# A gelu-times-half kernel: the first two tiles in pieces, later tiles in whole instructions, activations pinned in order

## Chip, cores, metric

One core of one Trainium2 chip. The metric is the device time of one execution in microseconds (us); lower is better. Every run below except two slow executions of one experiment is in the fast state, and only fast runs are compared. A ratio is the mean time of one kernel's fast runs over the mean of the kernel before's fast runs of the same rounds, on the same chip; it is not quite the ratio of the medians quoted beside it. The span of a profile, from its first to its last instruction, is some 2 us shorter than the time.

## The reference

```python
def setup_inputs():
    batch, seq, dim = (32, 512, 2048)
    return {'x': np.random.randn(batch, seq, dim).astype(np.float32)}

def reference(x):
    half_dim = x.shape[-1] // 2
    x1, x2 = x[..., :half_dim], x[..., half_dim:]
    gelu_x1 = 0.5 * x1 * (1 + erf(x1 / np.sqrt(2)))
    return (gelu_x1 * x2).astype(np.float32)
```

134.2 MB are read and 67.1 MB written, and there is one gelu and one product for each output element.

## The kernel before

The input is cut into 16 tiles. In a tile each of the 128 partitions holds R = 8 rows, so a load moves 8.39 MB (64 KB contiguous per partition) and a store 4.19 MB (32 KB per partition). There are two input and two output buffers. The gelu runs in place on the left half of the input tile (ACT), the product goes into the output tile (DVE). Loads are issued on the SP queue, stores on the ACT queue, except those of the last two tiles, which are on the SP queue behind the last load.

```python
R = 8
xpool = ctx.enter_context(tc.tile_pool(name="xpool", bufs=2))
opool = ctx.enter_context(tc.tile_pool(name="opool", bufs=2))

def load(i):
    x_tile = xpool.tile([P, R, dim], x.dtype, name="x_tile")
    nc.sync.dma_start(out=x_tile, in_=x_t[i])
    return x_tile

def store(queue, i, o_tile, rows):
    queue.dma_start(out=o_t[i][:, rows, :], in_=o_tile[:, rows, :])

ahead = [load(0), load(1)]
for i in range(n_tiles):
    x_tile = ahead.pop(0)
    o_tile = opool.tile([P, R, half], out.dtype, name="o_tile")
    last = i == n_tiles - 1
    for lo, hi in ((0, 1), (1, 2), (2, 4), (4, 8)) if last else ((0, 4), (4, 8)):
        rows = slice(lo, hi)
        nc.scalar.activation(
            out=x_tile[:, rows, :half], in_=x_tile[:, rows, :half], func=GELU
        )
        nc.vector.tensor_mul(
            out=o_tile[:, rows, :], in0=x_tile[:, rows, :half], in1=x_tile[:, rows, half:],
        )
        if last and hi % 4 == 0:
            store(nc.sync, i, o_tile, slice(hi - 4, hi))
    if not last:
        store(nc.sync if i == n_tiles - 2 else nc.scalar, i, o_tile, slice(0, R))
    if i + 2 < n_tiles:
        ahead.append(load(i + 2))
# ... launch code cut
```

The instructions pass a scheduler when the program is built. It may put an instruction of an engine ahead of another that was written earlier. The written order is therefore not always the order on the engine.

Of the kernel before, what the change touches and what calls it, by code (L numbers as in the profile page):

```python
# [1 line left out]

# [4 lines left out]

GELU = mybir.ActivationFunctionType.Gelu


@with_exitstack
def kernel(
    ctx: ExitStack,
    tc: tile.TileContext,
    x: bass.AP,
    out: bass.AP,
):






    nc = tc.nc
    P = nc.NUM_PARTITIONS

    x_flat = x.flatten_outer_dims()
    out_flat = out.flatten_outer_dims()
    n_rows, dim = x_flat.shape
    half = dim // 2  # L30

    R = 8
    x_t = x_flat.rearrange("(n p r) d -> n p r d", p=P, r=R)
    o_t = out_flat.rearrange("(n p r) d -> n p r d", p=P, r=R)
    n_tiles = x_t.shape[0]
# [9 lines that stand above are left out]
    def store(queue, i, o_tile, rows):  # L45
        queue.dma_start(out=o_t[i][:, rows, :], in_=o_tile[:, rows, :])

    ahead = [load(0), load(1)]
    for i in range(n_tiles):
        x_tile = ahead.pop(0)  # L50
        o_tile = opool.tile([P, R, half], out.dtype, name="o_tile")
        last = i == n_tiles - 1
        for lo, hi in ((0, 1), (1, 2), (2, 4), (4, 8)) if last else ((0, 4), (4, 8)):
            rows = slice(lo, hi)
            nc.scalar.activation(  # L55
                out=x_tile[:, rows, :half], in_=x_tile[:, rows, :half], func=GELU
            )
            nc.vector.tensor_mul(  # L58
                out=o_tile[:, rows, :],
                in0=x_tile[:, rows, :half],  # L60
                in1=x_tile[:, rows, half:],
            )
            if last and hi % 4 == 0:
                store(nc.sync, i, o_tile, slice(hi - 4, hi))
        if not last:
            store(nc.sync if i == n_tiles - 2 else nc.scalar, i, o_tile, slice(0, R))
        if i + 2 < n_tiles:
            ahead.append(load(i + 2))


# [1 line left out]
_INS = ['x']  # L72
_OUTS = [((32, 512, 1024), 'float32')]


# [23 lines left out]
```

## Time and profile before

| | before |
|---|---|
| time, median of the 3 runs given at the start | 471.6 us (471.53 to 471.65) |
| span of the profile | 470.1 us |
| DVE / ACT busy | 140.5 / 115.4 us |
| bytes over the span | 201.3 MB, 428 GB/s |
| in the middle (tiles 3 to 13) | 434 GB/s, 29.0 us a tile |

How to read it: busy shares tell little here, because ACT and DVE work in short bursts between landings (7.12 and 8.76 us in each 29.0 us of the middle). The question is whether the transfer engines ever stand still, and that is answered by the byte rate in windows cut where tiles land. The prediction below shows those lines.

### The profile page before, as it was taken

How to read it: one execution, taken by the hardware profiler on the slowest of the kernel's cores; microseconds unless marked ns; L12 is line 12 of the kernel's file. 1: busy time of each engine (PE TensorE's matmuls, PEld its weight loads, DVE VectorE, ACT ScalarE, POOL GpSimd, SP SyncE). 2: the span in 40 equal slices, each digit the busy share in tenths (PEclk: the TensorE clock that was granted, in tenths of full speed). 3: DMA queues.
4: the chain of work that ended last, by engine and by line, in shares of the span. 5: the costliest groups of instructions: out<-in, count | busy, mean ns of one | idle time of the engine just before them, and what ended most of it. 6: DMA issues, size and time to landing. Idle time of an engine off the chain costs nothing.

```text
span 470.1 us, 217 instructions
## 1 busy us (share of the span) xinstructions
DVE 140.5 (30%) x34; ACT 115.4 (25%) x35; POOL 0.2 (0%) x4
## 2 busy tenths in 40 slices
DVE  0070703307043070420705106061150601507042
ACT  1051406024060230603206032060410605105060
POOL 0000000000000000000000000000000000000000
DMA  8999999999999999999999999999999999999988
GB/s 357 446 446 357 443 449 446 402 443 449 402 446 441 435 457 404 432 418 485 407 424 421 488 407 413 432 488 407 402 443 482 413 402 443 472 424 402 480 380 346
DMA packets 4754, 201.35 MB, mean 428 GB/s; under 512 B 528, under 2 KB 528, under 8 KB 528
## 3 DMA queue, kind: packets, MB, share of 16 engines
q1 hardware_dynamic: 2736, 142.61, 70.5%
q10 hardware_dynamic: 2016, 58.72, 28.9%
q14 instruction: 2, 0.02, 0.0%
HBM read 134.22 MB, written 67.11 MB: 428 GB/s over the span
## 4 chain that ended last, share of the span: by engine, by line
DMA 77%; DVE 14%; ACT 7%; issue 0%; ACTq 0%; SPq 0%
DMA x_tile<-in_x_dram 77%; DVE o_tile L58 14%; ACT x_tile L55 7%; ACTq L94 0%; SPq L42 0%; ACTq L55 0%
## 5 line engine op out<-in xcount | busy, mean ns | idle before, releaser
L58 DVE TENSOR_TENSOR o_tile<-x_tile 128x4096 f32<-128x4096 f32 (+2 forms) x34 | 140.5, 4171 | 321.2 <-ACT x_tile L55 321.2
L55 ACT ACTIVATE x_tile<-x_tile 128x4096 f32<-128x4096 f32 (+2 forms) x34 | 114.2, 3407 | 341.0 <-DMA x_tile<-in_x_dram 341.0
L55 ACT ACT_TABLE_LOAD x1 | 1.3, 1283 | 0.7 <-PEq L83 0.7
L83 POOL MEMSET const-bfloat16-1.0<- 128x1 bf16 x1 | 0.1, 102 | 0.0
L83 POOL MEMSET const-uint8-127<- 128x1 uint8 x1 | 0.1, 102 | 0.0
L83 POOL MEMSET const-float32-0.0<- 128x1 f32 x1 | 0.1, 99 | 0.2 <-issue 0.2
L83 POOL MEMSET const-float32-1.0<- 128x1 f32 x1 | 0.1, 99 | 0.0
## 6 DMA issues: line engine op xcount, KB each, us to landing
out_dram<-o_tile ACTq DMA_DIRECT2D x14, 4096.0 KB, 41.6
out_dram<-o_tile SPq DMA_DIRECT2D x1, 4096.0 KB, 24.8
out_dram<-o_tile SPq DMA_DIRECT2D x2, 2048.0 KB, 8.0
x_tile<-in_x_dram SPq DMA_DIRECT2D x16, 45.4
```

The lines of the kernel that those rows point to most:

```text
L55: nc.scalar.activation(out=x_tile[:, rows, :half], in_=x_tile[:, rows, :half], func=GELU)
L58: nc.vector.tensor_mul(out=o_tile[:, rows, :], in0=x_tile[:, rows, :half], in1=x_tile[:, rows, half:],)
L83: nc = _bacc.Bacc("TRN2", target_bir_lowering=False, num_devices=1)
```

## The change

Its intent: compute and store sooner at the start by cutting the loads, the instructions and the stores of tiles 0 and 1 into pieces; then pay less fixed cost by covering a whole tile with one activation and one product; and keep each activation behind the store written ahead of it (`keep_in_program_order`, called the pin below).

```diff
-    ahead = [load(0), load(1)]
+    def load_pieces(i):
+        x_tile = xpool.tile([P, R, dim], x.dtype, name="x_tile")
+        for r in range(0, R, 4):
+            rows = slice(r, r + 4)
+            nc.sync.dma_start(out=x_tile[:, rows, :], in_=x_t[i][:, rows, :])
+        return x_tile
+
+    ahead = [load_pieces(0), load_pieces(1)]
     for i in range(n_tiles):
...
-        for lo, hi in ((0, 1), (1, 2), (2, 4), (4, 8)) if last else ((0, 4), (4, 8)):
+        pieces = last or i < 2
+        if last or i == 0:
+            steps = (0, 1), (1, 2), (2, 4), (4, 8)
+        else:
+            steps = ((0, 4), (4, 8)) if i == 1 else ((0, 8),)
+        for lo, hi in steps:
             rows = slice(lo, hi)
-            nc.scalar.activation(
-                out=x_tile[:, rows, :half], in_=x_tile[:, rows, :half], func=GELU
+            tc.keep_in_program_order(
+                nc.scalar.activation(
+                    out=x_tile[:, rows, :half], in_=x_tile[:, rows, :half], func=GELU
+                )
             )
...
-            if last and hi % 4 == 0:
-                store(nc.sync, i, o_tile, slice(hi - 4, hi))
-        if not last:
+            if pieces and hi % 4 == 0:
+                store(nc.sync if last else nc.scalar, i, o_tile, slice(hi - 4, hi))
+        if not pieces:
             store(nc.sync if i == n_tiles - 2 else nc.scalar, i, o_tile, slice(0, R))
```

## The prediction

> **What bounds the kernel now.** I read the page from the top: the busy shares of the engines, the slices, the queues, then the chain that ended last, and asked the windows for the byte rate stage by stage.
>
> From the page of the kernel before:
>
> ```profile
> DVE 140.5 (30%) x34; ACT 115.4 (25%) x35; POOL 0.2 (0%) x4
> ...
> DMA  8999999999999999999999999999999999999988
> ...
> HBM read 134.22 MB, written 67.11 MB: 428 GB/s over the span
> ...
> DMA 77%; DVE 14%; ACT 7%; issue 0%; ACTq 0%; SPq 0%
> ```
>
> No compute engine is busy a third of the time; the transfer engines are at 90% or more in all but the first and the last two slices. The chain gives DVE and ACT 21%, but that is a walk back through releases: it crosses them because a load is issued when a buffer comes free, not because the transfers stood still meanwhile. Whether they stood still is a question for the windows, cut where tiles land (columns: window, its length, DVE, ACT and POOL busy with counts, clock, DMA share, GB/s):
>
> ```profile
> 0.00:22.80 22.80, 0.00 (x0) 1.29 (x2) 0.20 (x4) 1.00 0.98 414
> 22.80:45.19 22.39, 8.76 (x2) 7.12 (x2) 0.00 (x0) 1.00 1.02 413
> ...
> 103.35:422.35 319.00, 96.37 (x22) 78.36 (x23) 0.00 (x0) 1.00 1.00 434
> 422.35:449.89 27.54, 8.76 (x2) 7.12 (x2) 0.00 (x0) 1.00 0.96 415
> 449.89:461.70 11.81, 9.08 (x4) 7.31 (x4) 0.00 (x0) 1.00 0.97 416
> 461.70:470.10 8.40, 0.00 (x0) 0.00 (x0) 0.00 (x0) 1.00 0.74 318
> ```
>
> The middle runs at 434 GB/s, tile after tile: 8.39 MB in and 4.19 MB out are 12.58 MB, over 434 that is 29.0 us, the spacing of the activations below. All 201.33 MB at 434 GB/s take 463.9 us of the 470.1 us span. So 6.2 us is everything that is not transfer at the middle's rate. The head: 414 x 22.8 + 413 x 22.39 = 18.7 MB by 45.19 us, which at 434 needs 43.1 us, so it costs 2.1 us. The other 4.1 us are at the end: some 2 us are the last wait for completion and the finish (the last store is issued at 461.7 and lands 7.6 us later, the shortest of the stores, at 469.3; the span ends 0.8 us after), and some 2 us are rates of 415 rather than 434 from 422 us on. These short windows count whole packets (64 KB on each of 16 engines is 1 MB), so the split is good to a microsecond or two.
>
> The buffers turn over like this (timeline: start, us, engine, line, op, count, idle before and releaser):
>
> ```profile
> 22.80 7.12 ACT L55 ACTIVATE x_tile<-x_tile 128x4096 f32<-128x4096 f32 x2 [20.79 <-DMA x_tile<-in_x_dram]
> 26.45 8.76 DVE L58 TENSOR_TENSOR o_tile<-x_tile 128x4096 f32<-128x4096 f32 x2 [26.45 <-ACT x_tile L55]
> 35.24 0.38 ACTq L46 DMA_DIRECT2D out_dram<-o_tile  x1
> 45.19 7.12 ACT L55 ACTIVATE x_tile<-x_tile 128x4096 f32<-128x4096 f32 x2 [15.27 <-DMA x_tile<-in_x_dram]
> ...
> 74.42 7.12 ACT L55 ACTIVATE x_tile<-x_tile 128x4096 f32<-128x4096 f32 x2 [22.10 <-DMA x_tile<-in_x_dram]
> ...
> 103.35 7.12 ACT L55 ACTIVATE x_tile<-x_tile 128x4096 f32<-128x4096 f32 x2 [21.81 <-DMA x_tile<-in_x_dram]
> ```
>
> Tile 0 lands at 22.8, its product is done 12.4 us later, and then load 2 and store 0 go out. Load 1 still has 10 us to run: the load queue is never empty. In the middle the next load has 29.0 - 12.4 = 16.6 us left when a buffer comes free. The idle time of ACT and DVE costs nothing.
>
> [...] load 2, against stores with half its packet size, took 29.2 us (45.19 to 74.42), or 287 GB/s, two thirds of 434; equal bytes would have given it about 217 while a store ran. [...]
>
> **The change part by part.**
>
> *Loads of tiles 0 and 1 in two pieces.* Two more issues at 0.33 us, ahead of any need; no byte more or less. The first piece is 4.19 MB, 9.7 us: from the head's 2.1 us it is through at 11.8. In the kernel before load 0 should be through at 2.1 + 19.3 = 21.4 and ACT starts at 22.8, so I add 1.4 us for completion: ACT starts at 13.2 instead of 22.8.
>
> *Steps of tile 0.* Activations of 1, 1 and 2 rows (1049, 1049 and 1895 ns, as the last tile has them) end near 17.1, the 2-row product of 2.29 us at 19.4. Store 0a goes out at 19.4; in the old kernel the first store went at 35.2. Rows 4 to 8 land at about 22.8 as before, then 3.6 + 4.4 us: store 0b and load 2 go at 30.9 instead of 35.2. That is 4.3 us earlier, into a queue that holds load 1 anyway.
>
> *The pinned activation.* The activation of rows 4 to 8 stays behind the issue of store 0a (19.4 to 19.8). Its data come at 22.8, so the pin costs nothing. For later tiles the store waits for a product that ends long before the next tile lands.
>
> *Sharing afterwards.* From 21 us stores take a third. Load 1a and store 0a (32 KB against 16 KB packets) run to about 36, load 1b and store 0b to about 50.4; tile 1 is finished at 51.8 + 8.1 = 59.9 (57.6 before). Store 1 now moves in 16 KB packets against load packets of 64 KB, four to one: load 2 is through near 74.6 and load 3 near 98.8, four us ahead of before (about 102). Store 1 ends there too, and from then on the ratio is two to one, 29.0 us a tile.
>
> *Whole-tile instructions.* [...] In sequence 15.7 us, where two overlapped pieces took 12.4: 3.3 us later for each store and each load, 13 tiles (2 to 14). [...] The next load has 29.0 - 15.7 = 13.3 us left at the issue, so none of the 3.3 us reaches the transfer engines. Even if a load had all of them to itself it would take 19.3 us, above 15.7. The output buffer is not a wait either: store i ends about when load i+2 lands, and product i+2 starts 7.0 us after that.
>
> *The end.* Last tile unchanged; store 14 sits on the load queue behind load 15, and stores 14 and 15 are 8.39 MB, 19.3 us of transfers after the last load, against 11.8 us of compute until the last issue. It was covered before (449.9 to 469.3 is 19.4) and is covered now.
>
> *Sum.* Bytes: 0. Head until the first byte: 0. The stretch of loads alone gets some 15 us shorter; the windows of 5 us from 5 to 35 average 430 GB/s against 434 mixed, so this is worth 15 x 4/434 = 0.14 us. [...] The end is shifted in phase: store 13 now ends with load 15, not 2 us ahead of it, and part of the 2 us of poorer rate there may come back or grow. I take a gain of 0.4 us as the middle: 471.6 - 0.4 = 471.2.
>
> **The rivals.** *A: the earlier start carries through.* If the head counted as latency, the 4.3 us by which load 2 goes earlier would come off (467.3), or the 9.6 us of ACT (462.0). For it: the chain has 21% compute. Against it: 418 to 434 GB/s in the windows while that compute runs, and the 463.9 us of bytes, which leave no room[...]. *B: the longer compute empties the load queue.* Then up to 3.3 us on 13 tiles, 43 us: 514. Against it: 13.3 us of queued load, and 19.3 against 15.7 in the worst case. *C: a wait for the output buffer.* Store 1's small packets end it late; product 3 would start at about 107 and store 1 ends near 99, a margin of 7 us; a miss would delay load 5's issue, still covered. About 471.5. *D: smaller descriptors lower the rate.* The stores' 32 KB packets run inside the 434, and only 25 MB are concerned; even 3% worse there is 1.7 us: 473. *E: the end loses its cover*, if phases shift so that an engine runs dry before the last store: 1 or 2 us, 473.
>
> **Range and chances.** The middle follows from a floor of 463.9 us, which the change cannot touch, with 6 to 7 us around it of which perhaps 2 can move. So 470.3 to 472.3 for 8 in 10: half a load packet's round at the low side, D and E in part at the high side. [...] Slower by over 2% (481) needs B in part: 2%. Within: 97%.
>
> **What would show it.** Right: first store near 19.4 us, activation of tile 0 near 13, load 2 at about 31, activations in the middle 29.0 us apart with 434 GB/s, whole-tile durations of 7.0 and 8.7 us, time to landing of loads down from 45.4 to about 42 and of stores near 42, load share unchanged; DMA row full from slice 2 to 38. Wrong: a spacing over 29.1 us, a window of the middle under 425 GB/s, DVE waiting on stores, or a last load that lands more than 3 us from 449 us. If the time falls below 469, my account of the head or of the end is wrong; if it rises above 474, rate or queue.

The sum came to a gain of 0.4 us, 471.6 - 0.4 = 471.2; the 0.4 was a guess at the middle.

The 15.7 us in sequence are 7.0 for the activation of a whole tile and 8.7 for its product. The trace of the kernel before gives the same as an estimate: activations of 2048 and 4096 elements take 1895 and 3608 ns, so 8192 take 3608 + 2 x 1713 = 7034; products take 2293 and 4422, so 4422 + 2 x 2129 = 8680. Two neighbouring activations of 4096 overlap a little (7.12 us for both). That sharing goes by packet size, four to one as well as two to one, is an estimate from load 2 of the kernel before (29.2 us, 287 of 434 GB/s). That the transfers can't go faster than the 434 GB/s of the middle (the "floor of 463.9 us") is an estimate too.

## The result

| | before | after |
|---|---|---|
| time, median (6 runs each) | 471.56 us (471.34 to 471.69) | 471.81 us (471.71 to 472.17) |
| ratio | | 1.0007, 95% interval 0.9994 to 1.002 |
| span of the profile | 470.1 us | 469.6 us |

The two kernels take the same time as far as these runs can tell.

From the page of the kernel after (busy time of the engines, the slices, the bytes, the chain):

```profile
DVE 140.0 (30%) x23; ACT 114.6 (24%) x24; POOL 0.2 (0%) x4
...
DMA  8999999999999999999999999999999999999998
...
HBM read 134.22 MB, written 67.11 MB: 429 GB/s over the span
...
DMA 70%; DVE 14%; ACT 12%; another core or an unknown queue 1%; ACTq 0%; issue 0%; SPq 0%
```

There are 22 fewer compute instructions, and the transfer row is as full as before. ACT's share of the chain rose from 7% to 12%, since the chain now runs through a whole-tile activation, and the time did not move.

The windows of the kernel after, cut where its tiles land (window, length, DVE, ACT and POOL busy with counts, clock, DMA share, GB/s):

```profile
0.00:22.73 22.73, 4.66 (x3) 5.08 (x4) 0.20 (x4) 1.00 0.95 392
22.73:52.20 29.47, 8.85 (x2) 7.23 (x2) 0.00 (x0) 1.00 1.03 445
...
129.62:420.04 290.42, 86.92 (x10) 70.29 (x10) 0.00 (x0) 1.00 1.00 433
420.04:449.37 29.33, 8.69 (x1) 7.03 (x2) 0.00 (x0) 1.00 0.95 411
449.37:461.20 11.83, 9.08 (x4) 7.31 (x4) 0.00 (x0) 1.00 1.01 436
461.20:469.60 8.40, 0.00 (x0) 0.00 (x0) 0.00 (x0) 1.00 0.75 322
```

Ten tiles take 290.42 us, 29.04 a tile at 433 GB/s; the kernel before takes 29.00 at 434. Compute work now lies in the first window, and the end has the same shape. The first window's 392 GB/s (414 before) is made good by the second: 22.0 MB are through by 52.20 us, which at 434 GB/s need 50.8 us. So the head costs 1.4 us against 2.1 before, a difference below what these windows resolve.

The timeline of the kernel after (start, us, engine, line, operation, count, idle before and releaser; ACTq and SPq are issues of transfers on the queue of ACT or SP):

```profile
12.89 3.80 ACT L69 ACTIVATE x_tile<-x_tile 128x1024 f32<-128x1024 f32 x3 [10.88 <-DMA x_tile<-in_x_dram]
...
19.05 0.38 ACTq L47 DMA_DIRECT2D out_dram<-o_tile  x1
...
30.84 0.36 ACTq L47 DMA_DIRECT2D out_dram<-o_tile  x1
...
100.62 7.03 ACT L69 ACTIVATE x_tile<-x_tile 128x8192 f32<-128x8192 f32 x1 [17.15 <-DMA x_tile<-in_x_dram]
107.68 8.69 DVE L73 TENSOR_TENSOR o_tile<-x_tile 128x8192 f32<-128x8192 f32 x1 [15.48 <-ACT x_tile L69]
...
129.62 7.03 ACT L69 ACTIVATE x_tile<-x_tile 128x8192 f32<-128x8192 f32 x1 [21.97 <-DMA x_tile<-in_x_dram]
...
449.37 7.31 ACT L69 ACTIVATE x_tile<-x_tile 128x1024 f32<-128x1024 f32 x4 [22.30 <-DMA x_tile<-in_x_dram]
```

The first activation starts at 12.9 us instead of 22.8 and the first store goes out at 19.05 instead of 35.24, yet the last load lands at about 449.3 us where it landed at 449.8 before. The head start of 16 us on the first store is gone by then, as the prediction said: it only changes the order in which the same bytes move.

### The profile page after: what moved, and what is told of

It reads as the page before. It is cut to its first block, busy times and chain, and to the rows that moved or that the text cites. A ratio compares the mean times of both kernels' runs of the same rounds, so it can differ in the third digit from the quotient of the medians.

```text
span 469.6 us, 203 instructions
## 1 busy us (share of the span) xinstructions
DVE 140.0 (30%) x23; ACT 114.6 (24%) x24; POOL 0.2 (0%) x4
## 3 DMA queue, kind: packets, MB, share of 16 engines
HBM read 134.22 MB, written 67.11 MB: 429 GB/s over the span
## 4 chain that ended last, share of the span: by engine, by line
DMA 70%; DVE 14%; ACT 12%; another core or an unknown queue 1%; ACTq 0%; issue 0%; SPq 0%
DMA x_tile<-in_x_dram 70%; DVE o_tile L73 14%; ACT x_tile L69 12%; ACTq L109 0%; SPq L53 0%; ACTq L47 0%; ACTq L69 0%
## 5 line engine op out<-in xcount | busy, mean ns | idle before, releaser
L73 DVE TENSOR_TENSOR o_tile<-x_tile 128x8192 f32<-128x8192 f32 (+3 forms) x23 | 140.0, 6094 | 321.1 <-ACT x_tile L69 321.1
L69 ACT ACTIVATE x_tile<-x_tile 128x8192 f32<-128x8192 f32 (+3 forms) x23 | 113.3, 4948 | 341.3 <-DMA x_tile<-in_x_dram 341.3
## 6 DMA issues: line engine op xcount, KB each, us to landing
out_dram<-o_tile ACTq DMA_DIRECT2D x12, 4096.0 KB, 42.4
x_tile<-in_x_dram SPq DMA_DIRECT2D x4, 4096.0 KB, 28.8
x_tile<-in_x_dram SPq DMA_DIRECT2D x14, 42.2
```

The lines of the kernel that those rows point to most:

```text
L69: nc.scalar.activation(out=x_tile[:, rows, :half], in_=x_tile[:, rows, :half], func=GELU)
L73: nc.vector.tensor_mul(out=o_tile[:, rows, :], in0=x_tile[:, rows, :half], in1=x_tile[:, rows, half:],)
```

## The experiments

The standing theory, T: the transfers never stand still in either kernel, so moving compute earlier or later changes nothing. The main rival, R: the head start gains some microseconds and the longer chain of a whole-tile instruction loses them again. Two parts done alone tell these apart.

### The head alone

```diff
-            steps = ((0, 4), (4, 8)) if i == 1 else ((0, 8),)
+            steps = (0, 4), (4, 8)
```

> Only the head of the change: tiles 0 and 1 in pieces, pinned activations; tiles 2 to 14 keep two instructions each. Theory T (the transfers never stand still, so neither part of the change can reach the end): 471.6, within 0.5 of the kernel before; the last load lands near 449, the middle runs 29.0 us a tile. Rival R (the head gains some 4 us and the longer chain of whole-tile instructions gives them back): the head alone would be near 467 to 468.

Measured: 472.08 us (471.86 to 472.12, 5 runs) against 471.45, ratio 1.0011 (0.9998 to 1.0023). The head gives no time, so there is nothing for the other part to give back. R falls.

### Whole-tile instructions alone

Made from the kernel before:

```diff
-        for lo, hi in ((0, 1), (1, 2), (2, 4), (4, 8)) if last else ((0, 4), (4, 8)):
+        for lo, hi in ((0, 1), (1, 2), (2, 4), (4, 8)) if last else ((0, 8),):
```

> Only whole-tile instructions, loads and stores as in the kernel before, the last tile in its four steps. T: 471.6, within 0.5; loads go out 15.7 us after a landing instead of 12.4, and their time to landing falls from 45.4 to about 42 us. R (3.3 us of longer chain is paid at least once): 475 or more, and as much as 515 if it is paid for every tile.

Measured: 478.72 us (478.53 to 479.03), ratio 1.0153 (1.014 to 1.0167). This is a miss for T: 7.3 us slower, not 0.5, and R's figure for this run (475 or more) was met. The timeline shows what was not intended:

```profile
101.19 7.03 ACT L55 ACTIVATE x_tile<-x_tile 128x8192 f32<-128x8192 f32 x1 [21.97 <-DMA x_tile<-in_x_dram]
108.25 8.69 DVE L58 TENSOR_TENSOR o_tile<-x_tile 128x8192 f32<-128x8192 f32 x1 [20.30 <-ACT x_tile L55]
130.19 7.03 ACT L55 ACTIVATE x_tile<-x_tile 128x8192 f32<-128x8192 f32 x1 [21.97 <-DMA x_tile<-in_x_dram]
130.21 16.12 ACTq L46 DMA_DIRECT2D out_dram<-o_tile  x2
```

The product of tile 3 ends at 116.9 us, but its store goes out at 130.2: the activation of tile 4, waiting for its load, stands ahead of the store in ACT's queue. (The last line merges this store with the next one, which goes out on time when the product of tile 4 ends, 16 us later.) The scheduler did this in three places. Without the pin, whole-tile instructions alone are a different program, so this run changed two things at once.

### The changed kernel without the pins

```diff
-            tc.keep_in_program_order(
-                nc.scalar.activation(
-                    out=x_tile[:, rows, :half], in_=x_tile[:, rows, :half], func=GELU
-                )
-            )
+            nc.scalar.activation(
+                out=x_tile[:, rows, :half], in_=x_tile[:, rows, :half], func=GELU
+            )
```

> The changed kernel without the pins. In the built program two activations of later tiles now stand ahead of the store of the tile before them (two pairs of activation, activation, store, store). T: the two stores go out some 20 us later and the product two tiles later waits some 8 us for its output buffer, but loads fill the transfers meanwhile: 471.8, within 1. R2 (the pin is what keeps the changed kernel from losing): each of the two displaced stores costs the 8 us or so that the product waits, 480 to 488.

Measured: 476.93 us (475.46 to 477.02, 4 runs), ratio 1.0107 (1.0093 to 1.0121). Both expectations miss: it costs 5.5 us, more than T allowed and less than R2 said. The timeline has the same mark (the first pair of the two):

```profile
216.88 7.03 ACT L68 ACTIVATE x_tile<-x_tile 128x8192 f32<-128x8192 f32 x1 [21.97 <-DMA x_tile<-in_x_dram]
216.90 16.12 ACTq L47 DMA_DIRECT2D out_dram<-o_tile  x2
```

DVE's waits for a store come to a single one of 16.3 us, at the last tile, so the cost in the middle is not a product that waits for its buffer.

### The transfers with next to no compute

```diff
-                out=x_tile[:, rows, :half], in_=x_tile[:, rows, :half], func=GELU
+                out=x_tile[:, rows, :2], in_=x_tile[:, rows, :2], func=GELU
```

This is made from the kernel before. The product is cut to the same two elements of each row, into two output tiles that are filled once at the start. Its output is wrong, which doesn't matter for the time.

> Transfers of the kernel before with next to no compute (two elements of each row are computed, the stores send fixed tiles: the result is wrong on purpose). This is the floor of the transfers with this order of loads and stores. T: within 1 us of the kernel before, 470.6 to 471.6. Rival C (compute is on the path, as the chain's shares of 21 per cent for DVE and ACT suggest): well below 460.

Measured: 478.60 us (478.39 to 479.39, 4 runs), ratio 1.0153 (1.0139 to 1.0167). With almost no compute, the kernel is 7 us slower. Compute is not on the path, so rival C falls; but "the bytes at 434 GB/s" is not something the transfers do by themselves: in this run, where each store goes out right after a landing, the time is longer.

So T was incomplete. To see what differs, I took the completion records from each trace: it holds 16 records of 4 bytes for each transfer, which I read as one from each of the 16 transfer engines when its part is done (the trace doesn't name the engines). For each load, the first and the last of the 16 (us):

```
kernel                    load 5           load 7           load 10          load 15
before                  159.6-160.7      217.6-218.7      304.6-305.7      448.4-449.5
after                   157.9-158.2      216.0-216.3      303.1-303.5      448.3-448.8
whole tiles, no pin     156.9-157.6      215.3-218.3      301.5-306.7      445.4-454.8
after without pins      158.0-158.5      216.0-216.5      302.2-304.4      446.6-452.8
next to no compute      167.3-170.0      225.4-229.1      312.6-317.9      450.3-456.1
```

In the two kernels the 16 engines finish each load within 1.1 us of each other, to the end. In the three slower runs they drift apart: 9.4 us between the first and the last at load 15 in the run with whole tiles alone, and 6.2 us without pins. A load counts as landed when its slowest engine is done (with whole tiles alone the records of load 15 come from 445.4 to 454.8 us, and the activation that waits for it starts at 455.24), and single packets get longer: in the trace of the kernel after, load packets of 64 KB take 2.42 us; in the run with whole tiles alone, 24% of them take over 2.5 us from 160 to 220 us, a few 0.6 us more, and after 300 us 2%. The spacing of loads by their last record is 29.6 us there instead of 29.0 ((454.8 - 188.8)/9, from load 6 to load 15); by their first record it is 28.8 ((445.4 - 186.1)/9).

So only a part of the lost time is byte rate in the middle. Counted from the packet records, the engines move 433.4 GB/s from 100 to 440 us in the kernel after, and 431.4, 430.5 and 430.1 in the three slower runs (in the order of the table), which is worth 1.6 to 2.6 us. A part at least as large lies at the end: from 440 us to the last packet an engine stands idle for 5.5, 3.1 and 3.8 us on the average, against 0.3 in the kernel after. The fast engines have moved all that is queued, while the last tile can be computed, and its stores issued, only when the slowest engine has brought its part. The windows of the end, the kernel after and then whole tiles alone:

```profile
440.00:469.60 29.60, 9.08 (x4) 7.31 (x4) 0.00 (x0) 1.00 0.92 395
440.00:476.50 36.50, 10.45 (x5) 7.31 (x4) 0.00 (x0) 1.00 0.81 346
```

A new theory, S: a late store lets the store queue run dry; after that the engines fall out of step and stay so. Rival W: the whole-tile instructions cost by themselves.

### Whole-tile instructions alone, with the pins

```diff
 # on top of the run with whole tiles alone
+            tc.keep_in_program_order(
                 nc.scalar.activation(
                     out=x_tile[:, rows, :half], in_=x_tile[:, rows, :half], func=GELU
                 )
+            )
```

> Whole-tile instructions alone, now with the activations pinned, so that no store stands behind a later activation. Theory S (the 7 us of the run with whole tiles alone came from its three stores that the scheduler put behind the next tile's activation, so that the store queue ran dry; once it has, the 16 transfer engines fall out of step and stay so): 471.6, within 0.7; the activations of the middle 29.0 us apart to the end, and the 16 completions of a load within about 1 us of each other to the end. Rival W (the whole-tile instructions themselves cost, by their later releases): 478 again.

Measured: 471.53 us (471.46 to 471.66) against 471.62, ratio 0.9998 (0.9985 to 1.0011). The pin alone takes 7.2 us off the same instructions. Store 3 goes out when its product ends, not at 130.2 us:

```profile
116.94 0.36 ACTq L46 DMA_DIRECT2D out_dram<-o_tile  x1
```

The engines finish load 15 within 0.4 us. W falls: whole-tile instructions, pinned, cost nothing and gain nothing.

### One late store, early enough

The kernel after, with activations on a scratch tile between the activation and the store of tile 6, to delay that one store and nothing else:

```diff
-        queue.dma_start(out=o_t[i][:, rows, :], in_=o_tile[:, rows, :])
+        d = queue.dma_start(out=o_t[i][:, rows, :], in_=o_tile[:, rows, :])
+        if i == 6:
+            tc.keep_in_program_order(d)
...
+            for _ in range(6 if i == 6 else 0):
+                tc.keep_in_program_order(
+                    nc.scalar.activation(out=scratch, in_=scratch, func=GELU)
+                )
             nc.vector.tensor_mul(
```

> The changed kernel with six activations on a scratch tile ahead of the store of tile 6, which goes out some 3 us later than before, while the store of tile 5 has about 9 us to run: the store queue is not dry. S: 471.8, within 0.5; no change of spacing or of the spread of the completions. Rival L (any late store costs): 1 us or more above the changed kernel.

Measured: 471.49 us (471.33 to 471.58), ratio 0.9996 (0.9983 to 1.0008). No cost, spread at load 15 of 0.6 us. But the run did not do what was expected of it:

```profile
204.22 0.34 ACTq L47 DMA_DIRECT2D out_dram<-o_tile  x1
```

Store 6 is only 0.7 us later than in the kernel after (203.55), not 3 us, so this says little about rival L. The next run settles it.

### One late store, the queue dry

The same with 15 in place of 6.

> The same with fifteen such activations: store 6 goes out some 20 us later, about 8 us after store 5 has landed, so the store queue is dry once, for one tile; loads go on (the next load is issued with several us in hand). S: 474 to 478; after tile 8 or so the spacing is 29.3 to 29.7 us instead of 29.0, the 16 completions of a load drift apart to 4 us and more, and the last tile's product waits for its output buffer. Rival B (transfers are busy with loads meanwhile, bytes alone count): 471.8, within 0.5.

Measured: 471.57 us (471.5 to 471.76), ratio 0.9999 (0.9986 to 1.0011). S misses clearly. Its timeline:

```profile
221.30 0.34 ACTq L47 DMA_DIRECT2D out_dram<-o_tile  x1
...
253.10 8.69 DVE L83 TENSOR_TENSOR o_tile<-x_tile 128x8192 f32<-128x8192 f32 x1 [14.29 <-DMA out_dram<-o_tile]
```

Store 6 goes out at 221.3 us, 17.8 us later than in the kernel after and 5 us after store 5 ended (216.4), so the queue was dry. A late store as such costs nothing: L falls here. From then on the products wait for their output buffers in 7 tiles (136.6 us of idle time in total in the list of waits, most of which DVE would have spent waiting for ACT), and even so the time is that of the kernel before. A dry queue and a wait for a buffer each cost nothing here: loads move on in the meantime. S falls, and what is left is when exactly the late store starts. In this run stores end 10.9 us after loads from then on (252.7 against 241.8). In the run without pins they ended 3.7 us after (247.9 against 244.2), in the run with whole tiles alone 3.6. On each engine a load packet and a store packet take turns: put into 16 back-to-back series, all 2,997 pairs of neighbouring packets of the kernel after from 100 to 440 us are one of each queue. One turn of a load packet (2.42 us, 64 KB) and a store packet (1.21 us, 32 KB) takes 3.63 us. In the kernel after, stores and loads end together; in the kernel before, stores end 3.6 us ahead of loads. In the run with next to no compute the first store ends 4.4 us (first engines, 54.1 against 49.7) to 6.0 us (last engines, 57.0 against 51.0) after load 1, which is not one turn: this run fits the theory below only loosely. Theory P: stores that end one turn after a load put the engines out of step; other distances don't.

### Thirteen and fourteen scratch activations

```diff
-            for _ in range(15 if i == 6 else 0):
+            for _ in range(13 if i == 6 else 0):
```

> As the run with fifteen scratch activations ahead of store 6, now thirteen: the store goes out at about 217.5 us, a little over 1 us after store 5 has landed, so that it misses one turn and each later store ends one turn (2.42 + 1.21 = 3.6 us) after a load, as in the run without pins (3.7 us there) and the run with whole tiles alone (3.6 us). Theory P (not the dry queue, but this phase of the ends of stores and loads puts the transfer engines out of step): 474 to 477, completions of a load drift apart to 4 us or more, spacing 29.3 to 29.6. Rival Q (one store that misses its turn does no harm, the cause lies elsewhere, in the order of two activations and two stores): 471.6, within 0.5, spread under 1 us.

> Fourteen scratch activations: store 6 goes out at about 219.4 us and misses two turns, so that stores end some 7.3 us after loads. P: no drift, as with 10.9 us in the run with fifteen: 471.6, within 0.5. If it drifts too, the phase that harms is broader than one turn; if neither this nor the run with thirteen does, P falls.

Measured, on one chip: with thirteen 476.51 us (475.74 to 476.94, 4 runs), ratio 1.0104 (1.0089 to 1.0119); with fourteen 471.26 us (471.13 to 471.5), ratio 0.9996 (0.9979 to 1.0013). The two programs differ in one scratch activation of 1.9 us that computes nothing of use. First the run with thirteen, then the run with fourteen:

```profile
217.47 0.34 ACTq L47 DMA_DIRECT2D out_dram<-o_tile  x1
...
244.54 7.03 ACT L75 ACTIVATE x_tile<-x_tile 128x8192 f32<-128x8192 f32 x1 [18.28 <-DMA x_tile<-in_x_dram]
...
274.40 7.03 ACT L75 ACTIVATE x_tile<-x_tile 128x8192 f32<-128x8192 f32 x1 [22.83 <-DMA x_tile<-in_x_dram]
```

```profile
219.43 0.34 ACTq L47 DMA_DIRECT2D out_dram<-o_tile  x1
...
243.53 7.03 ACT L75 ACTIVATE x_tile<-x_tile 128x8192 f32<-128x8192 f32 x1 [15.32 <-DMA x_tile<-in_x_dram]
...
272.46 7.03 ACT L75 ACTIVATE x_tile<-x_tile 128x8192 f32<-128x8192 f32 x1 [21.90 <-DMA x_tile<-in_x_dram]
```

A store that goes out 1.96 us earlier makes the rest slower: 29.9 us between tiles 8 and 9 against 28.9. The completion records say why it matters for good:

```
                    load 8               load 9               load 12              load 15
thirteen          242.6-244.2          272.0-273.7          360.5-363.8          448.9-452.9
fourteen          242.6-243.0          271.6-272.0          358.6-359.2          445.6-446.2
fifteen           241.5-241.8          270.5-270.8          357.5-358.0          444.5-445.0
without pins      243.8-244.2          272.9-273.7          359.6-363.7          446.6-452.8
```

P's forecast of the times held for both: harm with thirteen, none with fourteen (nor, before, with fifteen). But thirteen is not a clean test of "one turn". Three of the 16 engines missed two turns and 13 missed one: their first packets of store 6 start at 223.3 to 223.4 us and at 220.9 to 221.2. So the engines were out of step from the start (load 8 is spread over 1.6 us at once, store 6 over 2.5). In the run with next to no compute the first packets of store 0 are split in the same way, 13 engines at 27.5 to 27.9 us and three at 30.3 to 30.4. A rival that no run here excludes for these two is that the split does the harm, and not the distance. In the runs without pins and with whole tiles alone nothing is split at the late store; without pins, load 8 is still within 0.4 us and the drift comes over the next tiles.

It is shown that the moment of one store's start decides. On the late side the border is sharp: store 6 harms when it goes out at 216.9 (without pins) or 217.5 us, not at 219.4 or 221.3. On the early side nothing was run between 204.2 and 216.9. It is also shown by the records that engines that are out of step stay out (with thirteen, the first and the last are 1.6 us apart at load 8 and 4.0 at load 15). With thirteen they move 429.1 GB/s from 100 to 440 us instead of 433.4 and are idle for 2.1 us instead of 0.3 after that, about 5 us in all. Why the drift starts is not shown. That packets of loads and stores overlap on different engines is not enough: in the kernel before, of 1,245 load packets that had one to three store packets beside them on the average, one took over 2.45 us. This stays open.

### All stores in small packets

```diff
-        pieces = last or i < 2
+        pieces = True
...
-            if pieces and hi % 4 == 0:
-                store(nc.sync if last else nc.scalar, i, o_tile, slice(hi - 4, hi))
+            if hi % 4 == 0:
+                q = nc.sync if i >= n_tiles - 2 else nc.scalar
+                if lo == 0 and hi == 8:
+                    store(q, i, o_tile, slice(0, 4))
+                store(q, i, o_tile, slice(hi - 4, hi))
```

> The changed kernel with every store in two pieces of 16 KB packets against load packets of 64 KB, so that loads take four fifths and stores fall behind until the output buffers are full and the products wait for them. The load queue then runs dry now and then. Byte count alone: 472 to 473. S (a queue that runs dry costs): 476 to 486, DVE waits on stores in most tiles.

Measured: 484.18 us (483.94 to 484.54, 4 runs), ratio 1.0265 (1.025 to 1.0281). The list of waits of this run (engine, line, what it waited for: us in total, times, longest):

```profile
DVE o_tile L73 <- DMA out_dram<-o_tile: 208.5, 7, 35.3
```

Here the wait for the output buffer does cost, because it lasts so long (35 us) that the next load is issued only after the load before it has landed: load 5 has landed at 148.9 us, and the product that frees the buffer for load 6 ends at 158.4. There are six waits of 33 to 35 us and a short one; the whole run is 12.6 us longer, and how that divides among them and the end was not measured. Not all of S's reason applies (the engines stay within 0.8 us of each other, so it is not drift), but its range held. It also shows again how the queues share: load 3, against 16 KB store packets, took 24.1 us (76.4 to 100.5), or 348 GB/s, four fifths of 434; in the kernel after it took 24.2.

### The slack of the load queue

The prediction rests on 13.3 us of load still queued when a buffer comes free. Repeating the product of tiles 2 to 14 uses them up:

```diff
-            nc.vector.tensor_mul(
-                out=o_tile[:, rows, :],
-                in0=x_tile[:, rows, :half],
-                in1=x_tile[:, rows, half:],
-            )
+            for _ in range(2 if 2 <= i < n_tiles - 1 else 1):
+                nc.vector.tensor_mul(
+                    out=o_tile[:, rows, :],
+                    in0=x_tile[:, rows, :half],
+                    in1=x_tile[:, rows, half:],
+                )
```

> The changed kernel with the product of tiles 2 to 14 made twice: 15.7 + 8.7 = 24.4 us from a landing to the release, out of 29.0. If the slack of the load queue is what the prediction says (13.3 us), 4.6 us are left and nothing is lost: 471.8, within 0.7. Rival B (compute near the path): 5 us or more. If the store that now goes out 3 us before the one ahead of it ends misses a turn, P says 475 to 478 by drift, which the spread of the completions would show.

> The product made three times: 33.1 us from a landing to the release, and the next activation is pinned behind the store that waits for it, so tiles go through compute one after the other at 33.1 us instead of 29.0. The slack is used up: from tile 2 (lands at 76.4) the 13 tiles end at 76.4 + 13 x 33.15 = 507, the last tile's products near 516, the last two tiles' stores 8.39 MB after that: 529 in the profile, 531 in time (526 to 535). Idle transfers in every tile, mean near 381 GB/s.

Measured with two products: 487.53 and 487.69 us in the fast runs, two more at 502.71 and 506.81 (their cause was not looked into), ratio of the fast runs 1.0341. Three products: 558.02 us, ratio 1.1842. Both totals miss, with two products by more than the 5 us that rival B asked for, and the timelines say where. Two products:

```profile
133.73 7.03 ACT L69 ACTIVATE x_tile<-x_tile 128x8192 f32<-128x8192 f32 x1 [24.94 <-DMA x_tile<-in_x_dram]
...
423.73 7.03 ACT L69 ACTIVATE x_tile<-x_tile 128x8192 f32<-128x8192 f32 x1 [21.96 <-DMA x_tile<-in_x_dram]
430.79 8.69 DVE L74 TENSOR_TENSOR o_tile<-x_tile 128x8192 f32<-128x8192 f32 x1 [11.57 <-ACT x_tile L69]
452.78 7.31 ACT L69 ACTIVATE x_tile<-x_tile 128x1024 f32<-128x1024 f32 x4 [22.02 <-DMA x_tile<-in_x_dram]
453.87 17.50 DVE L74 TENSOR_TENSOR o_tile<-x_tile 128x1024 f32<-128x1024 f32 x5 [14.39 <-ACT x_tile L69]
463.72 8.00 SPq L47 DMA_DIRECT2D out_dram<-o_tile  x3
```

In the middle, 10 tiles take 290.0 us: 29.00 each with 24.5 us of compute from landing to release. The slack is as large as claimed, and 8.7 us more compute a tile cost nothing there. The 16 us are lost at two places that I had not thought of. Load 3 was quick (24.2 us, against small store packets), so load 3 had landed (100.5) before tile 2's release at 101.3 let load 4 go out, and load 4 ended at 133.3 instead of 129.2. And at the end the scheduler put the second product of tile 14 behind the first product of tile 15, so store 14 went out at 463.7 instead of 435.8 and the transfers stood still from 452 to 464. With three products the tiles are 33.7 us apart, not 33.15: 7.03 + 26.14 are compute and 0.5 are the store's issue (0.37) and hand-overs. That is 7 us of the miss over 13 tiles; the other 20 are again the last products in another order. The slack is shown by the middle of both runs, not by their totals.

No experiment gave a version that beats both kernels: 471.26 to 471.57 us in the four best are within the noise of the kernel before.

## Why the prediction was right, point by point

- *The bound.* Right for both kernels: 434 and 433 GB/s in the middle, with the transfer row full. What sets this rate was not shown. The head alone (1.0011) and whole tiles alone with pins (0.9998) show that each part is worth nothing, so it is not a sum of two terms that cancel.
- *Pieces of tiles 0 and 1.* The times came out within half a microsecond: first activation 13.2 told, 12.9 seen; first store 19.4 and 19.05; load 2 issued at 30.9 and 30.8; tile 1 done at 59.9 and 60.3.
- *Sharing by packets.* Four to one was right: load 3 took 24.2 us (76.44 to 100.62), 347 GB/s or 0.80 of 434. Loads 2 and 3 through at 74.6 and 98.8 told, their activations start 1.4 us later than that plus 0.4 (76.4 and 100.6). The first store packet came later than I took it: issued at 19.05, it moved at 23.4; in between 48 more load packets started, three on each engine. This changed nothing.
- *Whole-tile instructions.* 7.03 and 8.69 us, for 7.0 and 8.7 told; time to landing fell to 42.2 us for loads and is 42.4 for stores, as told. Their 3.3 us never reached the transfers.
- *The end.* Last load near 449, covered by 8.39 MB of stores, as told. The gain of 0.4 us was a guess at the phase of the end. The spans (469.5 to 470.0 in six runs of after, 469.5 to 470.4 in runs of before) and the time (0.25 us longer, not significant) do not show it.
- *The pinned activation.* "The pin costs nothing" is right, and this was the weakest step: I looked only at what the pin costs, not at what happens without it. Without it the same source is 5 us slower (1.0107), because the scheduler puts two activations ahead of the stores before them. The pin is the one part of the change with an effect on time; it keeps the whole-tile form from losing 5 to 7 us.
- *The rivals.* A and B fell as argued; the slack B needed is shown above. D and E, of 1 to 2 us each, are not seen in the result, but neither was tested by itself. C, a wait for the output buffer, costs nothing with fifteen scratch activations and up to 12.6 us with small stores, so "still covered" holds only as long as the wait ends before the load queue is empty. That bytes alone decide, on which the narrow range rested, is not generally true: four runs with the same bytes, and with each load issued well before the one ahead of it had landed, were 5 to 7 us slower. The changed kernel stayed in step, which I did not foresee as a condition; in this the range was luckier than its argument.

## What to carry to other kernels

With the transfer engines full, an earlier start of compute and fewer instructions were worth nothing here: check by the byte rate in windows, not by the shares of the chain. But look at the order in the built program, not only in the source: a store behind an activation that waits for a load starts at another moment, and here that moment alone decided between 471 and 477 us. Where two queues take turns, compare the first and last completion of the engines; if they drift apart, try to move a store by a microsecond or two, pin the order, and measure again.

## What the traces show of the transfers beside this

- Two queues in turn fell out of step here and lost rate: one store moved by 1.96 us changed the time from 471.26 to 476.51 us, with the spread of the 16 completions at the last load going from 0.5 to 4.0 us.
- From an issue to the first packet: the first packet of the first load of the kernel before came 0.63 us after the end of its issue (1.11 to 1.74 us) and 1.0 us after the start (0.73). Beside a busy queue it takes longer: a store issued on an idle queue moved after 4.3 us (32 KB load packets, kernel after: 19.05 to 23.4) or 7.2 us (64 KB, kernel before: 35.24 to 42.4); with thirteen scratch activations it was 3.4 us for the first engines and 6.0 us for the last.
- A program on one core moved 434 GB/s here, reading and writing HBM (134.22 and 67.11 MB). What bounds it there was not tested.
